# Gate and up of a feed-forward layer by seven block products instead of eight (Strassen's scheme), results through DRAM, then down

## The chip, the cores and the metric

One core of a Trainium2 chip runs the whole program. The metric is the device time in microseconds of one execution; the time before is the median of three executions.

## What is computed

One step of a hybrid decoder layer for 2048 prompt tokens and 32 sample tokens, model width 1024, feed-forward width 2816 (22 tiles of 128), all in float32. The change touches its last third:

```
x = x + g1 * (mixed @ w_out)
h = rms_norm(x, norm2_g) * (1 + sc2) + sh2
ff = silu(h @ w_gate) * (h @ w_up)
x = x + g2 * (ff @ w_down)
y = rms_norm(x, final_g)
```

A float32 product is made on TensorE from two reduced-precision pieces of each operand, hi (a copy rounded to fp32r by ScalarE) and lo (the rest, by a subtraction on GpSimd or VectorE): hi·hi + hi·lo + lo·hi, three matmuls for one.

## The kernel before, in words

`phase_out` (L1562) goes over the 16 token tiles of 128 in the order 8 to 15, then 0 to 7 (`order`, L1578). For a tile, `stage1` (48 matmuls `oz` of 512 columns, L1645 to L1647) makes the output projection; `stage1e` (L1658 to L1665) adds the residual, squares, and writes the normalised tile `oxn`; in the next round `stage2` transposes it (`oT`, L1673), scales it into `oh`, and splits it into hi and lo (L1684 to L1691). Tiles 0 to 7 stay in SBUF (`h2`), tiles 8 to 15 go to DRAM (`d_h2`). In the last round `next(ff)` puts the first gate and up work, `gate_up(0, 0)`, between the last `stage1` and the last `stage2`.

`phase_ff` goes over two halves of 1024 tokens and, in each, over the 22 ff tiles. For a tile, `gate_up` works on three chunks of tokens (256, 384, 384; 288 for the first chunk of the second half, with the sample tokens). For a chunk it makes two products of 8 blocks of the contraction and 3 matmuls each, that is 2 x 24 matmuls `fg` (L1908, L1909, L1911), then SiLU on ScalarE, a multiplication on VectorE (L1915), and the hi/lo split (L1916, L1917). The down product of the tile before, `down` (three matmuls `fd` of 512 columns for each of 16 accumulators, L1948 to L1950, and an addition on VectorE, L1957), stands between the chunks. Weights arrive in pieces of 256 KB through SyncE's queue and are split by `split_next` (L1857 ScalarE, L1858 GpSimd).

At the end of each half the accumulators are multiplied by g2 and the residual is added, ahead of the last sum (`pre`, L1986 VectorE and L1987 GpSimd, 128 x 1024 each). `last_sum`, `fin_rms` and `fin_out` then finish tile by tile; at the very end this is the list `LAST`. The order of instructions on each engine is the order in which the program writes them, and each engine takes its own strictly in that order. Each engine's DMAs are issued by SyncE in the order of the program too.

PSUM has two pools of four buffers: `R["a"]` for projections and gate/up, `R["b"]` for transposes and down.

Of the kernel before, what the change touches and what calls it, by code (L numbers as in the profile page):

```python
# [7 lines left out]
F32 = mybir.dt.float32  # L8
# [11 lines left out]
HT = 1024  # L20
LOG_G = [__import__("math").log1p(-(2.0 ** (-5.0 - h))) for h in range(NRH)]
# [75 lines left out]
def hybrid_step(ctx: ExitStack, tc: tile.TileContext, i: dict, o: dict):  # L97
# [57 lines left out]
    d_h2 = [dram.tile([DM, T + NS], F32R, name=f"d_h2{a}") for a in range(2)]  # L155
# [1403 lines left out]

    CH = [(0, 256), (256, 384), (640, 384)]  # L1560

    def phase_out(R, ff):  # L1562
# [5 lines left out]
        h_p = P("oh", 1)  # L1568
# [9 lines left out]
        order = list(range(8, 16)) + list(range(8))  # L1578
# [88 lines left out]
        def stage2(t):  # L1667
# [13 lines left out]
            if t < 8:  # L1681
                c = (t + 1) // 3
                hh, hl = (a[:, :, t * 128 - CH[c][0]:t * 128 - CH[c][0] + 128] for a in R["h2"][c])
                act.copy(hh, h)  # L1684
                pool.tensor_tensor(hl, h, f32(hh), ALU.subtract)
                return
            for g in range(2):
                hv = h[:, 4 * g:4 * g + 4]
                hh, hl = (R["gu"].tile([128, 4, 128], F32R, tag=f"g{a}", name=f"oh{a}") for a in range(2))
                act.copy(hh, hv)  # L1690
                pool.tensor_tensor(hl, hv, f32(hh), ALU.subtract)  # L1691
                for a, s in enumerate((hh, hl)):
                    later(d_h2[a][512 * g:512 * g + 512, t * 128:(t + 1) * 128].rearrange("(k p) n -> p k n", p=128), s)
# [3 lines left out]
        def half(tag, name):  # L1697
            return [R["gu"].tile([128, 4, 128], F32, tag=tag, name=name)[0:NS].rearrange("p k n -> p (k n)") for _ in range(2)]

        def sample0():  # L1700
            SM["g"] = half("g0", "g1s")
            SM["xs"] = half("g1", "oxs")
            for c in range(2):
                cs = slice(c * 512, c * 512 + 512)
                for b in range(NB):
                    dma(SM["g"][c][4 * b:4 * b + 4, :], d_g[1 + b:2 + b, 0, cs].to_broadcast([4, 512]))
                dma(SM["xs"][c], i["x_sample"].rearrange("b t d -> (b t) d")[:, cs])
# [26 lines left out]
        def sample1x():  # L1734
            for c in range(2):
                dve.tensor_scalar(SM["xn"][c], SM["x1"][c], SM["s3"][:, 4:5], None, ALU.mult)

        def sample2():
            xn = SM["xn"]
            pt = R["b"].tile([128, 512], F32, tag="b", name="oTs")  # L1740
            v = pt[:, 0:256].rearrange("p (k b t) -> p k b t", k=8, t=4)
            for k in range(8):
                pe.transpose(pt[:, k * 32:(k + 1) * 32], xn[k // 4][:, k % 4 * 128:k % 4 * 128 + 128], ident[0:NS, 0:NS])
            t, hh, hl = (R["wr"].tile([128, 4, 128], F32 if x == 0 else F32R, tag="g", name=f"ohs{x}").rearrange("p k n -> p (k n)")[:, 0:256]
                         .rearrange("p (k n) -> p k n", k=8) for x in range(3))
# [6 lines left out]
            for a, s in enumerate((hh, hl)):  # L1752
                dma(d_h2[a][:, T:T + NS].rearrange("(k p) n -> p k n", p=128), s)
# [398 lines left out]
```

## Time and profile before

| what | value |
|---|---|
| median of 3 executions | 3173.06 us (3171.83 to 3179.8) |
| profiled execution | 3173.09 us, of which its span 3171.3 us |
| mean granted TensorE clock | 0.965 |
| PE busy | 3086.2 us, 97% of the span |
| DVE / POOL / ACT busy | 1333.2 / 1255.7 / 944.9 us |
| on the chain that ended last | PE 85% of the span |

The profile lists each engine's busy time, then the chain of work that ended last. PE is TensorE, DVE VectorE, ACT ScalarE, POOL GpSimd, SP SyncE. An operation is written out<-in with its shape. Matmuls overlap in their records: what one costs is the distance from start to start, not its listed length. A time in square brackets behind a row is the idle time ahead of it and what ended it.

### The profile page before, as it was taken

What the parts mean: (1) busy time and instruction counts of PE and PEld (TensorE: products, weight loads), DVE (VectorE), ACT (ScalarE), POOL (GpSimd) and SP (SyncE); (2) the same over time, 40 slices, a digit from 0 to 9 for tenths busy, and PEclk for the clock granted to TensorE, in tenths of its full rate; (3) what the DMA queues carried; (4) which work ended last, traced back from release to release, by engine and by line L of the source; (5) the groups of instructions that cost most, each with busy time, mean ns of one, the idle gap of its engine ahead of it and who ended that gap; (6) DMA issues with size and microseconds to landing.
All of it is one profiled execution on the core that took longest, in us unless ns stands there. A gap on an engine that the chain in (4) does not pass through costs nothing.

```text
span 3171.3 us, 45654 instructions
## 1 busy us (share of the span) xinstructions
PE 3086.2 (97%) x17690; PEld 2747.4 (87%) x17690; DVE 1333.2 (42%) x2772; ACT 944.9 (30%) x1869; POOL 1255.7 (40%) x1093
## 2 busy tenths in 40 slices
PE   8999999999999997989999999999999999999997
PEld 4777888889999997768889999999998999999996
DVE  6424533124343334664552333333363344334447
ACT  5333422204444462463342111111123111111112
POOL 4546836302333342564343333333354333223337
PEclk9999999997898798999999999999999999999999
DMA  6555745627544428774642111121153111111122
GB/s 230 162 163 169 226 124 166 196 74 170 129 109 102 99 59 241 245 252 149 191 130 60 41 54 47 40 60 41 50 191 116 40 47 51 44 41 53 48 72 83
DMA packets 354035, 361.91 MB, mean 114 GB/s; under 512 B 36701, under 2 KB 266909, under 8 KB 350678
## 3 DMA queue, kind: packets, MB, share of 16 engines
q1 hardware_dynamic: 352888, 357.92, 38.2%
q8 instruction: 139, 2.28, 0.3%
q10 hardware_dynamic: 930, 1.07, 0.1%
q14 instruction: 78, 0.64, 0.1%
HBM read 274.41 MB, written 84.50 MB: 113 GB/s over the span
## 4 chain that ended last, share of the span: by engine, by line
PE 85%; DVE 3%; issue 3%; DMA 3%; POOL 2%; ACT 1%; SPq 0%; POOLq 0%; DVEq 0%; ACTq 0%
PE fg L1908 10%; PE fg L1909 10%; PE fg L1911 10%; PE fd L1949 5%; PE z L518 5%; PE fd L1950 5%; PE fd L1948 5%; PE z L519 5%; PE z L523 5%; PE aB L874 3%; PE aB L873 3%; PE aS L806 2%; PE aS L808 2%; PE aB L858 2%; PE oz L1645 1%
## 5 line engine op out<-in xcount | busy, mean ns | idle before, releaser
L1909 PE MATMUL fg<-h,g 128*128 128x384 f32 (+2 forms) x2112 | 653.1, 320 | 0.0
L1908 PE MATMUL fg<-h,g 128*128 128x384 f32 (+2 forms) x2112 | 652.0, 320 | 0.0
L1917 POOL TENSOR_TENSOR f<-sg,f 128x256 fp32r<-128x256 f32 x132 | 127.9, 969 | 948.1 <-ACT f L1916 948.1
L1957 DVE TENSOR_TENSOR acc<-fd,acc 128x512 f32<-128x512 f32 x640 | 437.2, 691 | 13.1 <-PE fd L1950 7.3
L1915 DVE TENSOR_TENSOR sg<-fg,sg 128x256 f32<-128x256 f32 (+1 forms) x132 | 68.5, 519 | 866.0 <-PE fg L1911 863.3
L1908 PEld LDWEIGHTS fg<-h,g 128*128 128x128 f32 x2112 | 397.5, 188 | 6.1
L1909 PEld LDWEIGHTS fg<-h,g 128*128 128x128 f32 x2112 | 397.1, 188 | 5.1
L1911 PE MATMUL fg<-h,g 128*128 128x384 f32 (+2 forms) x2112 | 374.8, 319 | 0.0
L1911 PEld LDWEIGHTS fg<-h,g 128*128 128x128 f32 x2112 | 340.2, 188 | 0.0
L518 PE MATMUL z<-w,hh 128*128 128x512 f32 x768 | 310.7, 405 | 2.0 <-ACT w L313 1.7
L519 PE MATMUL z<-w,hh 128*128 128x512 f32 x768 | 305.4, 398 | 0.9 <-DVE w L314 0.9
L1948 PE MATMUL fd<-d,f 128*128 128x512 f32 x704 | 275.2, 391 | 7.5 <-ACT acc L1955 3.4
L880 POOL TENSOR_TENSOR pl<-p,ph 128x512 fp32r<-128x512 f32 (+2 forms) x128 | 155.4, 1214 | 315.0 <-ACT ph L879 233.8
L1950 PE MATMUL fd<-d,f 128*128 128x512 f32 x704 | 276.1, 392 | 2.8 <-POOL f L1917 2.8
L1949 PE MATMUL fd<-d,f 128*128 128x512 f32 x704 | 276.2, 392 | 1.2 <-POOL d L1858 1.2
L1914 ACT ACTIVATE sg<-fg 128x256 f32<-128x256 f32 (+1 forms) x132 | 60.8, 460 | 664.9 <-PE fg L1911 664.9
L812 DVE CUSTOM_DVE_ANT_0 junk<-aS,mask 128x256 f32<-128x256 f32 (+1 forms) x384 | 121.1, 363 | 298.4 <-PE aS L808 297.2
L1858 POOL TENSOR_TENSOR g<-gr,g 128x512 fp32r<-128x512 f32 x176 | 229.3, 1325 | 0.0
L1916 ACT CAST f<-sg 128x256 fp32r<-128x256 f32 x132 | 63.0, 477 | 504.1 <-DVE sg L1915 504.1
L523 PE MATMUL z<-w,hl 128*128 128x512 f32 x768 | 193.1, 393 | 0.0
L518 PEld LDWEIGHTS z<-w,hh 128*128 128x128 f32 x768 | 147.0, 191 | 34.9 <-ACT w L313 2.1
L519 PEld LDWEIGHTS z<-w,hh 128*128 128x128 f32 x768 | 147.1, 192 | 31.7 <-DVE w L314 1.5
(337 smaller groups left out, 6103.9 us busy)
## 6 DMA issues: line engine op xcount, KB each, us to landing
raw<-in_w_in SPq DMA_DIRECT2D x96, 256.0 KB
gr<-in_w_gate SPq DMA_DIRECT2D x88, 256.0 KB
gr<-in_w_up SPq DMA_DIRECT2D x88, 256.0 KB
dr<-in_w_down SPq DMA_DIRECT2D x88, 256.0 KB
ar<-in_w_ada SPq DMA_DIRECT2D x32, 512.0 KB
d_qk<-g SPq DMA_DIRECT2D x64, 256.0 KB
v<-d_v SPq DMA_DIRECT2D x16, 1024.0 KB
sk<-in_cache_attn_k SPq DMA_DIRECT2D x56, 256.0 KB
```

The lines of the kernel that those rows point to most:

```text
L518: pe.matmul(ps, hh[:, k, :], hi[:, k, :], start=(k == 0), stop=False)
L519: pe.matmul(ps, hh[:, k, :], lo[:, k, :], start=False, stop=False)
L523: pe.matmul(ps, hl[:, k, :], hi[:, k, :], start=False, stop=(k == 7))
L880: (dve if gi in DV[h] else pool).tensor_tensor(lo[:, 0:off], p[:, 0:off], f32(hi[:, 0:off]), ALU.subtract)
L1858: (eng or pool).tensor_tensor(lo, t, f32(hi), ALU.subtract)
L1908: pe.matmul(ps[:, 0:w], wh, xh[:, k], start=(k == 0), stop=False)
L1909: pe.matmul(ps[:, 0:w], wh, xl[:, k], start=False, stop=False)
L1911: pe.matmul(ps[:, 0:w], ww[k // 4][1][:, k % 4], xh[:, k], start=False, stop=(k == 7))
L1948: pe.matmul(ps, f[0][:, tt], d[0][:, cs], start=(q == 0), stop=False)
L1949: pe.matmul(ps, f[0][:, tt], d[1][:, cs], start=False, stop=False)
L1950: pe.matmul(ps, f[1][:, tt], d[0][:, cs], start=False, stop=(q == len(ns) - 1))
L1957: dve.tensor_tensor(acc, ps, acc, ALU.add)
```

## The change

Gate and up become block products after Strassen (in Winograd's form, with seven products for eight). For each pair of ff tiles (11 pairs) and each pass over the tokens, the weight is seen as 2 x 2 blocks (two halves of the contraction, two ff tiles) and the activations as 2 x 2 blocks (two halves of the contraction, two blocks of tokens). Seven products of 4 x 3 = 12 matmuls each replace eight of 12. There are three passes over the tokens with blocks of 384, 384 and 272 columns (`NCH`; the last with 16 sample tokens in each block).

- In `phase_out` the tile order changes so that tiles come in pairs (t, t+3; in the last pass t, t+2). After a pair's second tile, `combine` makes four sums of 128 x 512 on DVE, and `blocks` splits seven operands into hi and lo (ScalarE, GpSimd). Four of them for pass 0 stay in SBUF; all others go to DRAM (`d_B`), fourteen writes of 256 KB for a pair (six in pass 0). The last three of a pair are split one round later (`rest`).
- `g_build` makes the weight's seven operands for each pair, pass and matrix: four sums of 128 x 512 on DVE and seven splits. The subtraction of a split is on GpSimd; in the last pass two of seven are on VectorE. They are built five products ahead. The weights are read once a pass, three times in all instead of twice.
- `product` combines the seven products with seven additions on DVE that read PSUM, for each matrix; the four results go through SiLU and a multiplication, and are written to DRAM as `d_ff`.
- Down follows when gate and up are done: it reads `d_ff` and w_down back, splits them (`d_build`), and adds two ff tiles at a time in PSUM (6 matmuls for one addition into the accumulator instead of 3). The finish of each half is as before, without gate and up between its steps.
- `gate_up(0, 0)` no longer stands ahead of the last `stage2`.

```diff
+NCH = (384, 384, 272)
-        order = list(range(8, 16)) + list(range(8))
+        order = [0, 3, 1, 4, 2, 5, 6, 9, 7, 10, 8, 11, 12, 14, 13, 15]
+        def combine(b11, b21, b12, b22, t1, t2, t4):
+            dve.tensor_tensor(t1, b12, b11, ALU.subtract)
+            dve.tensor_tensor(t2, b22, t1, ALU.subtract)
+            dve.tensor_tensor(b12, b22, b12, ALU.subtract)
+            dve.tensor_tensor(t4, b21, t2, ALU.subtract)
+            return [b11, t2, b12, t1, b21, t4, b22]
...
+        def g_build(s):
+            q, idx = divmod(s, 14)
+            x, w = divmod(idx, 2)
...
+            if x == 1:
+                s1, s2 = tmp(1), tmp(2)
+                dve.tensor_tensor(s1, a21, a22, ALU.add)
+                dve.tensor_tensor(s2, s1, a11, ALU.subtract)
+            if x == 2:
+                dve.tensor_tensor(tmp(3), a11, a21, ALU.subtract)
+            if x == 4:
+                dve.tensor_tensor(tmp(4), a12, GT[w, 2], ALU.subtract)
...
+            act.copy(hi, src)
+            eng = dve if q >= 2 * NP_ and x in (2, 5) else pool
+            eng.tensor_tensor(lo, src, f32(hi), ALU.subtract)
...
+        def product(s):
...
+            for k in range(4):
+                pe.matmul(ps, hi[:, k], xh[:, k], start=(k == 0), stop=False)
+                pe.matmul(ps, hi[:, k], xl[:, k], start=False, stop=False)
+            for k in range(4):
+                pe.matmul(ps, lo[:, k], xh[:, k], start=False, stop=(k == 3))
+            put_off()
+            if x == 0:
+                act.copy(t, ps)
+            elif x < 3:
+                dve.tensor_tensor(t, ps, PT[w, x - 1], ALU.add)
+            else:
+                dve.tensor_tensor(v, ps, PT[w, (2, 0, 2, 1)[x - 3]], ALU.add)
+                if x == 3:
+                    dve.tensor_tensor(t, ps, t, ALU.add)
+                if w == 0:
+                    act.activation(SG[out], v, AF.Silu)
+                else:
+                    def end():
+                        dve.tensor_tensor(sg, v, sg, ALU.mult)
+                        later(d_ff[f][:, t0:t0 + m], sg[:, 0:m])
...
+        for s in range(14 * NG):
+            product(s)
+            while built[0] < s + 1 + LEAD:
+                build()
...
+                for x in range(2):
+                    d, f = DO[q, 2 + x, c], DO[q, x, t // 4]
+                    pe.matmul(ps, f[0][:, tt], d[0], start=(x == 0), stop=False)
+                    pe.matmul(ps, f[0][:, tt], d[1], start=False, stop=False)
+                    pe.matmul(ps, f[1][:, tt], d[0], start=False, stop=(x == 1))
```

Three places where the order of instructions matters below. First TensorE's at the end of `phase_out`; `oz` is the last projection, `oT` the transposes of the last tile, `fg` gate and up. Before:

```order
L1645 MATMUL oz<-wo_14043,m_16363 128x512
L1646 MATMUL oz<-wo_14044,m_16363 128x512
L1647 MATMUL oz<-wo_14043,m_16364 128x512
L1908 MATMUL fg<-h_14832,g_16300 128x256
L1909 MATMUL fg<-h_14833,g_16300 128x256
```

and in the changed kernel:

```order
L1645 MATMUL oz<-wo_14069,m_16465 128x512
L1646 MATMUL oz<-wo_14070,m_16465 128x512
L1647 MATMUL oz<-wo_14069,m_16466 128x512
L1673 MATMUL oT<-ident,oxn 128x128 x8
L1980 MATMUL fg<-B_14870,op_14863 128x384
```

The transposes of the last tile now follow its projection at once; the first gate product stands behind them.

Second SyncE's DMAs at the same place in the changed kernel; `B40` to `B61` are activation blocks of pass 0, `op` and `B70` hold the last pair's blocks for the last pass, and `raw3` is the first piece that the up matrix needs for its second operand (with index 3 of the products):

```order
L110 DMA B60_16659<-d_B00_71 128x1536
L110 DMA B61_16660<-d_B01_72 128x1536
L110 DMA d_x1_70<-x1_16529 128x1024
L110 DMA d_B20_75<-op00_14855 128x4x128
L110 DMA d_B21_76<-op01_14856 128x4x128
L110 DMA d_B20_75<-op10_14857 128x4x128
...
L110 DMA d_B21_76<-B71_16662 128x4x128
L110 DMA d_x1_70<-x1_16630 128x1024
L110 DMA raw3_16734<-in_w_up 128x4x256
L110 DMA raw4_16735<-in_w_gate 128x4x256
```

The piece `raw3` stands behind six reads of 768 KB and fourteen writes of 256 KB.

Third VectorE's order in the last pass of the changed kernel; L1901 to L1906 are sums of weight blocks, L1911 the low half of a split, L1990 and L1997 additions from PSUM, L2007 the multiplication behind SiLU:

```order
L2007 TENSOR_TENSOR sg_23255<-fc_23274,sg_23255 128x272
L1997 TENSOR_TENSOR sg_23296<-fg_23282,fu_23099 128x272
L1901 TENSOR_TENSOR s1_23299<-raw1_14853,raw3_16734 128x512
L1902 TENSOR_TENSOR s2_23300<-s1_23299,raw1_14853 128x512
L1997 TENSOR_TENSOR fc_23318<-fg_23305,fu_23117 128x272
L1904 TENSOR_TENSOR s3_23320<-raw0_14852 128x512
L1911 TENSOR_TENSOR op01_14856<-s3_23320,op00_14855 128x512
L2007 TENSOR_TENSOR sg_23296<-fc_23318,sg_23296 128x272
L1904 TENSOR_TENSOR s3_23340<-raw1_14853 128x512
L1911 TENSOR_TENSOR op11_14858<-s3_23340,op10_14857 128x512
```

Where VectorE had one operation on gate and up for each 24 pairs of matmuls, it now has about two operations for each product of 12 matmuls, and over half of them take both operands from SBUF.

## Rows read from the trace of the kernel before

**Rows 1.** The page: the span, and each engine's busy time, share and instructions.

```profile
span 3171.3 us, 45654 instructions
PE 3086.2 (97%) x17690; PEld 2747.4 (87%) x17690; DVE 1333.2 (42%) x2772; ACT 944.9 (30%) x1869; POOL 1255.7 (40%) x1093
```

**Rows 2.** Busy time by stretch of the span: start and end us, length, then busy us (and instructions) of PE, PEld, DVE, ACT and POOL, the granted clock, the DMA share, GB/s. Two stretches of the feed-forward stage in the first half, then the change of halves and one behind it.

```profile
2200.00:2300.00 100.00, 100.00 (x578) 94.09 (x578) 37.51 (x57) 17.79 (x36) 30.93 (x27) 1.00 0.16 48
2300.00:2400.00 100.00, 97.83 (x548) 91.28 (x547) 61.86 (x70) 25.30 (x50) 60.17 (x46) 1.00 0.58 188
2400.00:2500.00 100.00, 96.60 (x529) 89.11 (x528) 29.41 (x43) 26.04 (x55) 31.78 (x34) 0.98 0.22 69
2600.00:2700.00 100.00, 100.00 (x564) 93.42 (x564) 38.61 (x60) 16.69 (x36) 30.07 (x29) 1.00 0.16 48
```

**Rows 3.** Instructions of PE in order of time (start us, length us, engine, line, operation): the first gate product of 256 columns, the transposes behind its 48 matmuls; a group of 24 matmuls of 384 columns, the 18 of 512 behind it and the next; a group of 24 of 288 columns and what follows.

```profile
1637.76 0.28 PE L1908 MATMUL fg<-h,g 128*128 128x256 f32 x1
1643.41 1.03 PE L1673 MATMUL oT<-ident,oxn 128*128 128x128 f32 x8
...
1908.45 0.33 PE L1908 MATMUL fg<-h,g 128*128 128x384 f32 x1
1912.61 0.39 PE L1948 MATMUL fd<-d,f 128*128 128x512 f32 x1
1916.73 0.33 PE L1908 MATMUL fg<-h,g 128*128 128x384 f32 x1
...
2400.66 0.29 PE L1908 MATMUL fg<-h,g 128*128 128x288 f32 x1
2403.86 0.39 PE L1948 MATMUL fd<-d,f 128*128 128x512 f32 x1
```

**Rows 4.** Groups of instructions by line and shape, the whole span: engine, operation, shapes and count, then busy us, mean ns of one, and the idle time before them.

```profile
L1957 DVE TENSOR_TENSOR acc<-fd,acc 128x512 f32<-128x512 f32 x640 | 437.2, 691 | 13.1 <-PE fd L1950 7.3
L1915 DVE TENSOR_TENSOR sg<-fg,sg 128x384 f32<-128x384 f32 x88 | 49.1, 558 | 645.1 <-PE fg L1911 642.5 <-ACT sg L1914 2.7
L1915 DVE TENSOR_TENSOR sg<-fg,sg 128x288 f32<-128x288 f32 x22 | 10.0, 456 | 111.6 <-PE fg L1911 111.6
L1659 DVE TENSOR_TENSOR x<-x,ox 128x512 f32<-128x512 f32 x32 | 37.0, 1157 | 1.1
L1727 DVE TENSOR_TENSOR x1s<-x1s,oxs 32x512 f32<-32x512 f32 x2 | 1.4, 678 | 0.1
L1858 POOL TENSOR_TENSOR g<-gr,g 128x512 fp32r<-128x512 f32 x176 | 229.3, 1325 | 0.0
L1691 POOL TENSOR_TENSOR oh<-oh,oh 128x512 fp32r<-128x512 f32 x16 | 24.4, 1546 | 52.2 <-ACT oh L1690 52.2
L1987 POOL TENSOR_TENSOR acc<-acc,fx 128x1024 f32<-128x1024 f32 x16 | 40.3, 2526 | 10.6 <-DVE acc L1986 8.1 <-DVE acc L1957 2.4
L1857 ACT CAST g<-gr 128x512 fp32r<-128x512 f32 x176 | 100.3, 617 | 0.4 <-DMA gr<-in_w_gate 0.4
```

**Rows 5.** Instructions in order of time at the end of the first half: a multiplication of the accumulators on DVE beside GpSimd's work, the GpSimd instruction that ran at its start, and the same multiplication with less beside it.

```profile
2338.67 3.36 DVE L1986 TENSOR_TENSOR acc<-acc,g2b 128x1024 f32<-128x1024 f32 x1
...
2338.55 2.39 POOL L1987 TENSOR_TENSOR acc<-acc,fx 128x1024 f32<-128x1024 f32 x1
...
2362.84 1.35 DVE L1986 TENSOR_TENSOR acc<-acc,g2b 128x1024 f32<-128x1024 f32 x1
```

**Rows 6.** Instructions in order of time for one tile of `phase_out`: the transposes of one tile and of the next, the normalised tile between them, and GpSimd's two splits.

```profile
1501.60 1.03 PE L1673 MATMUL oT<-ident,oxn 128*128 128x128 f32 x8
1513.90 1.03 PE L1673 MATMUL oT<-ident,oxn 128*128 128x128 f32 x8
...
1508.93 0.75 DVE L1665 TENSOR_SCALAR oxn<-x,os 128x1024 f32<-128x1024 f32 x1 [2.26 <-POOL os L1664]
...
1504.83 3.00 POOL L1691 TENSOR_TENSOR oh<-oh,oh 128x512 fp32r<-128x512 f32 x2 [6.57 <-ACT oh L1690]
```

**Rows 7.** Instructions in order of time at the end of `phase_out`: the last transposes but one, the last matmul of the projection, the last normalised tile.

```profile
1632.47 1.66 PE L1673 MATMUL oT<-ident,oxn 128*128 128x128 f32 x8 [2.27 <-DVE oxn L1665]
1637.53 0.40 PE L1647 MATMUL oz<-wo,m 128*128 128x512 f32 x1
...
1641.90 0.76 DVE L1665 TENSOR_SCALAR oxn<-x,os 128x1024 f32<-128x1024 f32 x1 [1.97 <-POOL os L1664]
```

**Rows 8.** Busy time by stretch, as rows 2: ten microseconds in which the blocks of the second half were read (rows of 1 to 1.5 KB), and four in which transposed tiles were written (rows of 512 bytes).

```profile
2370.00:2380.00 10.00, 10.00 (x54) 9.32 (x53) 3.12 (x5) 4.35 (x9) 7.39 (x8) 1.00 1.06 374
1564.00:1568.00 4.00, 4.00 (x19) 3.32 (x18) 2.04 (x3) 1.80 (x6) 0.18 (x1) 1.00 0.96 305
```

**Rows 9.** Instructions of PE behind the change of halves, in order of time: an idle time and the matmuls of 384 columns that came after it.

```profile
2410.12 0.50 PE L1948 MATMUL fd<-d,f 128*128 128x512 f32 x1 [3.36 <-ACT acc L1955]
2412.06 0.52 PE L1908 MATMUL fg<-h,g 128*128 128x384 f32 x1
2414.30 0.43 PE L1909 MATMUL fg<-h,g 128*128 128x384 f32 x1
```

**Rows 10.** Instructions in order of time at the end: the last sums' first matmul, the first multiplication of its result, and VectorE's last operation.

```profile
3118.05 0.39 PE L1948 MATMUL fd<-d,f 128*128 128x512 f32 x1
3121.19 0.69 DVE L1998 TENSOR_TENSOR ft<-fd,g2b 128x512 f32<-128x512 f32 x1 [2.32 <-PE fd L1950]
3166.40 1.28 DVE L2028 SCALAR_TENSOR_TENSOR fsp<-acc,fs,fgb 128x1024 f32<-128x1024 f32 x1 [0.72 <-POOL fs L2020]
```

**Rows 11.** Busy time by stretch, as rows 2: ten microseconds of the attention stage.

```profile
970.00:980.00 10.00, 10.00 (x56) 9.80 (x56) 2.67 (x9) 3.28 (x6) 2.57 (x2) 0.50 1.02 202
```

More of the change, by code (lines that the diff above doesn't have):

```diff
@@ L1680, in stage2 @@
                         dve.tensor_scalar(h[:, kk], v, modA[1][:, kk, 0:1], modB[1][:, kk, 0:1], ALU.mult, ALU.add)
[L1681 to L1685, printed above, removed]
-                return
[L1687 to L1693, printed above, removed]
+            p = min(t // 6, 2)
@@ L1695, in phase_out @@
         SM = {}
-        def half(tag, name):
-            return [R["gu"].tile([128, 4, 128], F32, tag=tag, name=name)[0:NS].rearrange("p k n -> p (k n)") for _ in range(2)]
         def sample0():
[L1701 to L1707, printed above, removed]
+            SM["g"], SM["xs"] = (r[0:NS] for r in R["raw"][0:2])
@@ L1814, in phase_out @@
         stage2(order[15])
+        rest()
+        put_out()
         settle()
@@ new lines, in phase_ff @@
+        yield
+        build()
+        yield
+        P, close_g = group("left")
+        more = P("fmore", 1)
+        BO += [[more.tile([128, 4, 384], F32R, name=f"B{x}{a}") for a in range(2)] for x in range(4, 8)]
+        R["late"] = [[a[:, :, 128 * x:128 * x + 128] for a in BO[7]] for x in range(3)]
+        for x in range(4, 7):
+            b_load(0, x)
+        yield
+        Q, close_gw = group("right")
+        gw = Q("fgw", 1)
+        RAW += [gw.tile([128, DM], F32, name=f"raw{x}") for x in range(3, 6)]
@@ new lines, in phase_ff @@
+        for s in range(14 * NG):
+            q, idx = divmod(s, 14)
+            product(s)
+            if s == 8:
+                b_load(1, 0)
+            if idx == 8 and q == NP_:
+                b_load(2, 0)
+            while built[0] < s + 1 + LEAD:
+                build()
+            if s == 14 * (NG - 1):
+                for x in range(4):
+                    d_raw(0, x)
+        put_off()
+        settle()
+        close_g()
+        R["close_B"]()
+        P, close_down = group("right")
@@ L1926, in phase_ff, with down @@
-        gate_up(0, 0)
-        yield
-        P, close_right = group("right")
-        accp = P("facc", 1)
-        accs = [accp.tile([128, DM], F32, name=f"acc{t}") for t in range(8)]
-        acs = one.tile([64, DM], F32, name="accs")
-        def down(ns, t, c, raw=False):
-            f0 = seqf[ns[0]][1]
+        while built[0] < 14 * NG + 8:
+            build()
+        bank = [0]
+        def down(q, t, c, raw=False):
+            bank[0] ^= 1
+            ps = R["ab"[bank[0]]].tile([128, 512], F32, tag="ab"[bank[0]], name="fd")
@@ L1936, in down @@
             cs = slice(c * 512, c * 512 + 512)
[L1937 removed]
             if t == 8:
[L1939 removed]
+                for x in range(2):
                     for a in range(2):
[L1941 to L1942 removed]
+                        pe.matmul(ps[0:64], DO[q, "s", x], DO[q, 2 + x, c][a], start=(x == 0 and a == 0), stop=(x == 1 and a == 1))
@@ L1957, in down @@
                 dve.tensor_tensor(acc, ps, acc, ALU.add)
-        spare = [one.tile([128, DM], F32, name=f"fsp{i}") for i in range(2)]
         X = {"as": spare[0][0:NS], "g2s": spare[1][0:NS]}
```

438 lines of the change are left out of this document (247 added, 191 removed).

## The prediction
> **What bounds the kernel now.** I read the page's head first: TensorE is busy 97% of the span [rows 1], so the time is its instructions plus few gaps. The stretches come next [rows 2]: in the feed-forward stage it is busy throughout at the full clock, DVE a third of the time, POOL a third, the DMA engines 16%. The order in time [rows 3] gives the price of a matmul, from start to start: 24 of 384 columns take 1912.61 - 1908.45 = 4.16 us, 0.1733 each; 18 of 512 take 4.12, 0.229 each; 24 of 288 take 3.20, 0.1333 each; 48 of 256 take 5.65, 0.1177 each. So columns are what is paid, and fewer of them is time saved as long as the other engines keep up. They have to do far more here, so the rest of the argument is about them.
>
> **Gate and up on TensorE.** Before, 22 tiles x 48 matmuls x 0.1177 and x 0.1333, and 22 x 192 x 0.1733: 124 + 141 + 732 = 997 us. Now 33 rounds (a round is one pair of ff tiles in one pass) x 168 matmuls, of 384, 384 and 272 columns. For 272 I estimate 0.1255, between the groups of 256 and 288 [rows 3]. 1848 x (0.1733 + 0.1733 + 0.1255) = 872 us. **-125 us.** Down has 2112 matmuls of 512 columns in both, at no change. A round lasts 168 x 0.1733 = 29.1 us in the first two passes, 21.1 us in the third. Of the 48 matmuls taken to be on the path before, the 8.3 us of the last `gate_up` stood inside the final chain of DVE, POOL and ACT (3118.05 to the end, 53 us [rows 10]), where I let its loss save 3 only: **+5**.
>
> **The sums and splits of a round, passes 0 and 1.** DVE: 8 weight sums with both operands in SBUF. Such an operation takes 0.678 us alone (L1727) and 1.157 on average beside POOL (L1659) [rows 4]; I take 1.157. Then 14 additions from PSUM at 0.558 and 4 multiplications of 384 columns at 0.558 + 0.47 for the same delay: 9.3 + 7.8 + 4.1 = 21.2 us. POOL: 14 splits at 1.325 (L1858) to 1.546 (L1691) = 18.6 to 21.6. ACT: 14 copies at 0.617 and six smaller operations, some 12. All below 29.1, so I cost them at nothing; TensorE covers them, with 7 us to spare. Without that cover each microsecond over 29.1 would cost 22 us.
>
> **The third pass.** TensorE gives only 21.1 us. DVE now has 12 operations with two SBUF operands, four of them low halves: 12 x 1.157 = 13.9; 14 additions from PSUM at 0.456 (L1915 of 288 columns, for 272) = 6.4; 4 multiplications at 0.456 + 0.47 = 3.7. Together 24.0 us, 2.9 more than TensorE, x 11 = 32; the five operands built ahead and eight PSUM buffers hide some 8 of it once. **+24** (0 if DVE is not slowed: 16.3 us; upper end in the rivals). Why DVE is slow beside POOL, the order in time shows [rows 5]: the multiplication that began at 2338.67, just behind a POOL addition of 2.39 us, took 3.36 us, one with less beside it 1.35; the difference is the rest of the POOL instruction. The Trainium skill (SBUF — State Buffer, SBUF: two separate sides) speaks against this change: VectorE with two SBUF inputs and GpSimd take turns on a shared port pair, an exclusive lock held for the whole instruction. Rows 5 agree. By it alone the round's lock time would be 10 x 1.325 + 12 x 0.678 + 4 x 0.456 = 23.2 us, some 2 over TensorE, and the sum 9 us less than with my 24.0.
>
> **`phase_out`.** A tile's round is 12.3 us, from 1501.60 to 1513.90; its normalised tile is ready 8.1 us after the transposes [rows 6], so 4.2 us are spare. A pair's second tile now has, ahead of that, four DVE sums (2.7 to 4.6 us) and four splits on POOL instead of two (+3.1 us at 1.546), partly beside each other: some 5.9, so 1.7 us of waiting for each of 7 pairs. In the last round the transposes come 2.7 us earlier (one group of 12 matmuls) and already waited 2.27 [rows 7]; 3 us more. **+15** (0 if DVE and POOL overlap wholly; 35 if transfers come late too: a pair moves 6.7 MB in 24.6 us where 305 GB/s [rows 8] gives 22).
>
> **Entry into gate and up.** Before, TensorE went from the last projection straight into 48 gate matmuls [rows 3, 7]. Now it waits for the normalised tile until 1641.9 + 0.8 [rows 7], 5 us; after the transposes it has two products, then the third and fourth need POOL and a weight piece. POOL must first split the last pair's seven blocks: 3 us for scaling and the first sums, then 7 x 1.546 = 10.8, so to about 1657. SyncE cannot issue `raw3` before the writes of these blocks, and if transfers land in the order of issue it follows 4.7 MB of reads at 374 GB/s (12.6 us), 3.7 MB of writes at 305 (12 us) [rows 8] and 0.5 MB of the residual: 1665. With two sums and a copy the fourth product starts at about 1669, against 1645 without waits: 24 us, and the first matmuls after it come at the lower clock. That costs some 2 us: after an idle time of 3.36 us, 7 of 384 columns took 2.24 us, 0.32 each [rows 9]. **+27** (18 if `raw3` does not queue behind the writes, 38 if all reads and writes run at 250 GB/s).
>
> **Between the stages.** At a pass change 9.4 MB of blocks arrive over some 50 us at 374 GB/s where each is used 29 us after it is asked for: nothing. `d_ff`, and weights read a third time, add up to 2.9 MB a round, 100 GB/s: nothing, at the DMA shares of rows 2. Into down: the last three splits of the first pair and new buffers, **+4** (1 to 10).
>
> **The finish of the halves.** `pre` puts on each tile a multiplication on DVE (1.35 alone) and a POOL addition of 2.53 us [rows 4, 5], beside a split of 1.33: 5.2 us one after the other. Before, this had 33 us of matmuls for eight tiles, and still cost: 548 + 529 matmuls where 571 + 564 would be usual [rows 2], 57 x 0.176 = 10 us. Now it has 8 x 2.74 = 21.9 us. DVE ends them 20 us late and the next round, at some 3.2 us a tile with output and splits, 25 us late; TensorE, with eight PSUM buffers at most four tiles (11 us) ahead, loses 14, and 3 to its clock. 17 us, that is **+7** net (-5 to 15). Second half: 8 x 5.2 + 5.6 for the sample tile = 47 against 23.7 on TensorE, and the final chain waits for DVE's end: **+22** (8 to 30; before, gate and up covered it).
>
> **The sum.** -125 + 5 + 24 + 15 + 27 + 4 + 7 + 22 = -21. From the profiled execution's 3173.09, which is the median's 3173.06 within 0.1: **3152 us**, 0.7% faster. The unknowns add up to some 25 either way: 3130 to 3178 for this case.
>
> **Rivals.**
> *The other engines keep up.* The sums then wait little: third pass 0 instead of 24, entry 19. 3152 - 24 - 8 = 3120. For it: DVE alone would need 16.3 us of 21.1, and operands are built ahead. Against: rows 5, and the mean of L1659.
> *DVE waits a whole POOL instruction at each split.* Third pass: 16.3 + 10 x 1.325 = 29.6 us a round, (29.6 - 21.1) x 11 - 7 = 87 instead of 24: 3215, slower. It decides from 25.8 us a round on, where the third pass costs 45 and the gain is gone. For it: in-order DVE sits between POOL's splits, and the low halves wait for ACT's copy. Against: 14 additions from PSUM need no lock and can lie beside POOL.
> *Waiting TensorE runs at 1.2 GHz.* In a stretch of the attention stage it was listed busy throughout, at a clock of 0.50 [rows 11]. If four rounds of the third pass ran so, at 0.1255 x 0.32 / 0.1733 = 0.232 us for a matmul, 39 us a round: 4 x (39 - 24) = +60, 3212. The Trainium skill (TensorE: Matmul & The Clock Gate, A second HAM failure mode: psum-queue depth-cycling) tells of such a case, where small waits between groups let the clock fall again and again. Against: at 2300 to 2400 the clock stayed at 1.00 with 98% busy [rows 2].
> That the eighth product is still made can be excluded: in the order of instructions there are 5544 gate and up matmuls, 3 x 1848, where 6336 were.
>
> **How the numbers follow.** About 0.3% (9.5 us) is what a measurement of this kernel can tell from no change. My forecast has 0.50 (0.37 of it below 3163.6, 0.13 within), the first rival 0.25, the second 0.16, the third 0.09. Faster 0.62, same 0.13, slower 0.25. For 8 in 10 the range goes from 3105, a little under the first rival, to 3205; the two slow ones begin where the gain ends, so about half of their 0.25 lies inside.
>
> **What would show it.** Right: `fg` in 5544 matmuls at 0.173 and 0.125 from start to start; rounds of 29 us in passes 0 and 1 with TensorE busy, 24 in pass 2 with DVE never idle and its sums at 1.1 us; an idle time of about 20 us ahead of the fourth product, ended by a DMA; TensorE waiting for DVE or POOL at the end of both halves. Wrong: rounds of over 30 us in the first passes; pass 2 at 21 (first rival) or over 26 (second); a granted clock below 0.9 in pass 2 (third); waits of over 3 us for each pair in `phase_out`; or transfers late at the pass changes.

## The result, and the profile after

The changed kernel takes 3146.86 us (median of five executions, 3145.01 to 3154.42), the kernel before beside it 3171.83: a ratio of 0.9927, 95% interval 0.9906 to 0.9949. The forecast was 3152. So the sum came out 5 us too high; single terms are further off, and the profile shows which.

The head of the page first, to be set against [rows 1]: TensorE lost 792 matmuls and 105 us, DVE gained 443 us of work and GpSimd 363.

```profile
span 3145.0 us, 46998 instructions
PE 2981.4 (95%) x16898; PEld 2631.0 (84%) x16898; DVE 1776.3 (56%) x3271; ACT 1143.0 (36%) x2215; POOL 1618.9 (51%) x1279
```

The stretches next (columns as [rows 2]): the first passes, the third pass, the change to down, the end of the first half, and the round ahead of the last sums.

```profile
1900.00:2000.00 100.00, 100.00 (x577) 100.00 (x576) 68.25 (x89) 36.50 (x70) 68.81 (x50) 1.00 0.41 132
2400.00:2500.00 100.00, 96.65 (x734) 93.05 (x733) 88.89 (x133) 43.77 (x89) 64.18 (x44) 1.00 0.41 114
2580.00:2600.00 20.00, 16.92 (x75) 13.25 (x74) 5.23 (x5) 11.57 (x22) 12.06 (x10) 1.00 0.74 277
2800.00:2820.00 20.00, 10.55 (x35) 7.26 (x34) 19.10 (x15) 3.34 (x7) 16.91 (x8) 0.69 0.41 131
3060.00:3080.00 20.00, 19.15 (x84) 14.83 (x82) 19.83 (x17) 0.00 (x0) 20.00 (x11) 1.00 0.36 106
3080.00:3100.00 20.00, 13.81 (x49) 9.71 (x49) 15.01 (x11) 1.20 (x2) 18.66 (x8) 0.83 0.14 40
```

Passes 0 and 1 are what was forecast: TensorE busy throughout, 577 matmuls in 100 us, DVE at 68%. In the third pass 734 matmuls stand where the price of 0.1255 gives 797. At 2800 to 2820 there are 35 of 88.

A profile is one execution, and the place where a stage begins moves between executions. So stages are compared by their own length. The summary of the output projection on TensorE (line, count, min/median/max ns, first and last start), for the kernel before, then for the changed one:

```profile
L1645 PE MATMUL oz<-wo,m x256: 387/389/774, 1420.9 to 1637.1; 128*128 128x512 f32 x128
L1647 PE MATMUL oz<-wo,m x256: 388/389/628, 1421.3 to 1637.5; 128*128 128x512 f32 x128
```

```profile
L1645 PE MATMUL oz<-wo,m x256: 387/389/776, 1412.8 to 1651.8; 128*128 128x512 f32 x128
L1647 PE MATMUL oz<-wo,m x256: 387/389/628, 1413.3 to 1652.3; 128*128 128x512 f32 x128
```

Up to its first matmul the changed kernel was 8.1 us ahead, in a part of the program that both share; experiments with the same code there began anywhere from 1410.8 to 1428.3. From first to last it took 239.5 us for 216.6. With that, the differences by stage (us, + is slower):

| term | forecast | measured | from |
|---|---|---|---|
| matmuls of gate and up | -125 | -122 | 0.1740 each in passes 0 and 1 for 0.1733 |
| last gate_up in the final chain | +5 | +8 | final chain 50.1 us in both |
| third pass | +24 | +16 | 248.3 us for 1848 x 0.1255 = 231.9 |
| phase_out | +15 | +23 | 239.5 - 216.6 |
| entry | +27 | +36 | 1652.5 to 1699.6, with 11.4 us of work in it |
| into down | +4 | +3 | two waits on PE, 2.4 and 0.7 |
| first half's finish | +7 | +3 | 56 matmuls short x 0.2285 = 12.8, less the 10 of before |
| second half's finish | +22 | +14 | 37.8 us for a round of 23.8 |
| sum | -21 | -19 | spans -26.3, without the 8.1 ahead of it -18.2 |

**phase_out's end.** In the last round, in order of time: ACT, POOL, DVE (two rows), PE. In brackets, the idle time before the instruction and what ended it.

```profile
1650.62 0.62 ACT L1711 CAST op<-oh 128x512 fp32r<-128x512 f32 x1 [5.73 <-DMA d_B<-op]
...
1651.59 1.29 POOL L1712 TENSOR_TENSOR op<-oh,op 128x512 fp32r<-128x512 f32 x1 [5.28 <-DMA d_B<-op]
...
1652.92 1.36 DVE L1680 TENSOR_SCALAR oh<-oT,modA,modB 128x128 f32<-128x128 f32 x4 [5.82 <-POOL op L1712]
1659.50 0.75 DVE L1665 TENSOR_SCALAR oxn<-x,os 128x1024 f32<-128x1024 f32 x1 [2.22 <-POOL os L1664]
...
1660.31 1.97 PE L1673 MATMUL oT<-ident,oxn 128*128 128x128 f32 x8 [7.66 <-DVE oxn L1665]
```

Read upwards, TensorE waited 7.66 us for the normalised tile; DVE had stood 5.82 us at the activations of the tile before, whose buffer the split still read; POOL and ACT had waited 5 us to split, since the operand buffer was not yet written out. The last three blocks of a pair use the buffers of its first three. My estimate had the sums and splits, not this wait: from the first projection to the last, ACT has 37 us of it and POOL 33. The wait of 7.66 us itself stands behind the last projection, so the table has it under the entry.

The first wait for an operand buffer ends at 1552.6. Ahead of that, behind each of the first four pairs, TensorE waits 1.64 to 1.68 us for the normalised tile, with no such wait in front of it; for example:

```profile
1470.82 1.09 PE L1673 MATMUL oT<-ident,oxn 128*128 128x128 f32 x8 [1.68 <-DVE oxn L1665]
```

After 1552 TensorE's waits for this tile are 2.13, 3.65, 0.96 and 4.14 us.

**The entry.** The third and the fourth product, the sum that the fourth waits for, and SyncE's issues (x8 is eight in a row, from the first start to the last end):

```profile
1673.29 0.69 PE L1980 MATMUL fg<-B,op 128*128 128x384 f32 x1 [5.84 <-ACT op L1909]
1692.64 0.69 PE L1980 MATMUL fg<-B,op 128*128 128x384 f32 x1 [14.75 <-ACT op L1909]
...
1690.52 0.69 DVE L1901 TENSOR_TENSOR s<-raw,raw 128x512 f32<-128x512 f32 x1 [17.94 <-DMA raw<-in_w_up]
...
1664.42 13.58 SPq L110 DMA_DIRECT2D d_B<-op  x8
1678.10 5.38 SPq L110 DMA_DIRECT2D d_B<-B  x6
1684.51 0.71 SPq L110 DMA_DIRECT2D raw<-in_w_up  x1
```

The chain is the forecast one: `raw3` behind the writes. It is issued 32.2 us after the last projection, the product starts 40.4 us after it, where I had 31.5, since the writes wait for POOL, and POOL's splits of the last pair ended 22.7 us after it instead of 19.5. TensorE's granted clock was 0.57 over 1680 to 1700; the twelve matmuls of the fourth product took 4.0 us at the lower level, 1.2 GHz, for 2.1 at 2.4.

**The third pass.** Groups of DVE in 2350 to 2550 (columns as [rows 4]), then part of one round in order of time, DVE and POOL:

```profile
L2007 DVE TENSOR_TENSOR sg<-fc,sg 128x272 f32<-128x272 f32 x34 | 26.8, 790 | 1.2 <-ACT sg L2002 0.8
L1906 DVE TENSOR_TENSOR s<-raw,s 128x512 f32<-128x512 f32 x18 | 25.3, 1408 | 0.0
L1904 DVE TENSOR_TENSOR s<-raw 128x512 f32<-128x512 f32 x18 | 12.2, 680 | 0.0
L1911 DVE TENSOR_TENSOR op<-s,op 128x512 fp32r<-128x512 f32 x18 | 14.7, 814 | 13.6 <-ACT op L1909 13.6
L1997 DVE TENSOR_TENSOR fc<-fg,fu 128x272 f32<-128x272 f32 x26 | 11.3, 433 | 0.9 <-PE fg L1983 0.9
```

```profile
2425.84 0.68 DVE L1904 TENSOR_TENSOR s<-raw 128x512 f32<-128x512 f32 x1
...
2431.22 1.39 DVE L1906 TENSOR_TENSOR s<-raw,s 128x512 f32<-128x512 f32 x1
2432.54 0.43 DVE L1990 TENSOR_TENSOR fu<-fg,fu 128x272 f32<-128x272 f32 x1
2432.89 1.42 DVE L1906 TENSOR_TENSOR s<-raw,s 128x512 f32<-128x512 f32 x1
...
2430.77 2.99 POOL L1911 TENSOR_TENSOR op<-s,op 128x512 fp32r<-128x512 f32 x2 [3.10 <-ACT op L1909]
2433.72 3.45 POOL L1911 TENSOR_TENSOR op<-raw,op 128x512 fp32r<-128x512 f32 x2
```

A sum takes 0.68 us alone (2425.84) and 1.4 beside a POOL split; the two of 1.39 and 1.42 stand beside POOL's splits, and the addition from PSUM between them keeps its 0.43. Lengths of neighbours overlap: the operation at 2432.54 is 0.43 long and the next starts 0.35 later.

**The end.** The first multiplication of the accumulators, the first one behind the last sums, and DVE's last operation, as [rows 10]:

```profile
3057.10 1.22 DVE L2146 TENSOR_TENSOR acc<-acc,g2b 128x1024 f32<-128x1024 f32 x1
...
3094.91 1.27 DVE L2159 TENSOR_TENSOR ft<-fd,g2b 128x512 f32<-128x512 f32 x2
...
3140.23 1.28 DVE L2189 SCALAR_TENSOR_TENSOR fsp<-acc,fs,fgb 128x1024 f32<-128x1024 f32 x1 [0.72 <-POOL fs L2181]
```

From 3094.91 to the span's end it is 50.1 us, and from 3121.19 to 3171.3 [rows 10] it was 50.1 as well: taking a whole `gate_up` out of that chain saved nothing.

### The profile page after: what moved, and what is told of

It is laid out like the page before. It is cut to its first block, busy times and chain, and to the rows that moved or that the text cites. A ratio compares the mean times of both kernels' runs of the same rounds, so it can differ in the third digit from the quotient of the medians.

```text
span 3145.0 us, 46998 instructions
## 1 busy us (share of the span) xinstructions
PE 2981.4 (95%) x16898; PEld 2631.0 (84%) x16898; DVE 1776.3 (56%) x3271; ACT 1143.0 (36%) x2215; POOL 1618.9 (51%) x1279
## 4 chain that ended last, share of the span: by engine, by line
PE 77%; POOL 6%; issue 5%; DVE 4%; DMA 4%; SPq 1%; ACT 1%; POOLq 0%; ACTq 0%; DVEq 0%
PE fg L1983 8%; PE fg L1980 8%; PE fg L1981 8%; PE z L521 5%; PE z L522 5%; PE z L526 5%; PE fd L2110 4%; PE fd L2111 4%; PE fd L2109 4%; PE aB L877 3%; PE aB L876 3%; PE aS L809 2%; PE aS L811 2%; POOL op L1911 2%; PE aB L861 1%
## 5 line engine op out<-in xcount | busy, mean ns | idle before, releaser
L1980 PE MATMUL fg<-B,op 128*128 128x384 f32 (+1 forms) x1848 | 579.0, 323 | 25.7 <-ACT op L1909 25.7
L1981 PE MATMUL fg<-B,op 128*128 128x384 f32 (+1 forms) x1848 | 576.0, 321 | 0.0
L1911 POOL TENSOR_TENSOR op<-s,op 128x512 fp32r<-128x512 f32 x242 | 336.6, 1405 | 261.7 <-ACT op L1909 219.1
L1980 PEld LDWEIGHTS fg<-B,op 128*128 128x128 f32 x1848 | 349.2, 189 | 30.1 <-ACT op L1909 29.7
L1983 PE MATMUL fg<-B,op 128*128 128x384 f32 (+1 forms) x1848 | 370.4, 322 | 1.1
L1981 PEld LDWEIGHTS fg<-B,op 128*128 128x128 f32 x1848 | 349.6, 189 | 0.0
L1983 PEld LDWEIGHTS fg<-B,op 128*128 128x128 f32 x1848 | 306.1, 188 | 5.3 <-POOL op L1911 4.7
L2051 POOL TENSOR_TENSOR op<-raw,op 128x512 fp32r<-128x512 f32 x132 | 188.9, 1447 | 209.8 <-ACT op L2050 196.2
L2118 DVE TENSOR_TENSOR acc<-fd,acc 128x512 f32<-128x512 f32 x304 | 207.8, 689 | 154.8 <-PE fd L2111 154.5
L2110 PE MATMUL fd<-op,op 128*128 128x512 f32 x704 | 278.2, 395 | 16.5 <-POOL op L2051 16.5
L2109 PE MATMUL fd<-op,op 128*128 128x512 f32 x704 | 277.8, 395 | 10.8 <-DVE ft L2159 5.3
L1911 POOL TENSOR_TENSOR op<-raw,op 128x512 fp32r<-128x512 f32 x176 | 261.1, 1499 | 52.0 <-ACT op L1909 51.9
L2111 PE MATMUL fd<-op,op 128*128 128x512 f32 x704 | 277.4, 394 | 0.0
L1909 ACT CAST op<-s 128x512 fp32r<-128x512 f32 x264 | 160.3, 620 | 245.8 <-DVE s L1902 167.2
L2050 ACT CAST op<-raw 128x512 fp32r<-128x512 f32 x176 | 101.8, 621 | 306.1 <-issue 212.2
L2002 ACT ACTIVATE sg<-sg 128x384 f32<-128x384 f32 (+1 forms) x132 | 65.4, 495 | 323.1 <-DVE sg L1997 323.0
L521 PEld LDWEIGHTS z<-w,hh 128*128 128x128 f32 x768 | 146.5, 191 | 35.0 <-ACT w L316 2.1
```

The source lines that it names most:

```text
L521: pe.matmul(ps, hh[:, k, :], hi[:, k, :], start=(k == 0), stop=False)
L1911: eng.tensor_tensor(lo, src, f32(hi), ALU.subtract)
L1980: pe.matmul(ps, hi[:, k], xh[:, k], start=(k == 0), stop=False)
L1981: pe.matmul(ps, hi[:, k], xl[:, k], start=False, stop=False)
L1983: pe.matmul(ps, lo[:, k], xh[:, k], start=False, stop=(k == 3))
L2051: (dve if idx in (3, 7) else pool).tensor_tensor(lo, src, f32(hi), ALU.subtract)
```

## The experiments

Stage lengths in the profiled executions, us: `phase_out` from its first to its last projection; from there to the first matmul of 272 columns; the third pass to the first down matmul; from there to the span's end.

| kernel | phase_out | entry, passes 0 and 1 | third pass | down | median |
|---|---|---|---|---|---|
| changed kernel | 239.5 | 680.1 | 248.3 | 564.4 | 3146.9 |
| e1 early piece | 240.3 | 664.7 | 248.2 | 565.8 | 3134.7 |
| e2 all splits on POOL | 239.3 | 679.4 | 256.6 | 564.7 | 3158.0 |
| e3 no sums in pass 2 | 239.8 | 678.6 | 232.2 | 562.9 | 3133.0 |
| e4 half the writes | 235.5 | 667.9 | 248.3 | 564.2 | 3135.4 |
| e5 six buffers in turn | 233.2 | 678.5 | 248.1 | 565.8 | 3141.4 |
| e6 sums twice | 239.3 | 700.0 | 248.2 | 565.5 | 3171.9 |
| e8 scaled down weights | 240.3 | 681.5 | 248.1 | 521.7 | 3105.9 |
| e10 three together | 233.4 | 662.3 | 248.1 | 521.6 | 3084.0 |
| e11 three, mended | 240.0 | 660.8 | 248.1 | 521.1 | 3088.6 |
| e12 six splits on DVE | 239.6 | 678.5 | 255.6 | 566.1 | 3159.5 |
| e13 turn shifted | 232.6 | 663.9 | 248.1 | 521.0 | 3091.5 |

Lengths of stages that an edit does not touch agree within 3.2 us, mostly within 1; medians carry the shifts of the earlier stages besides, so small effects are read from the lengths.

**e1.** A buffer of its own for `raw3`, issued ahead of the blocks' reads:

```
+        R["raw3"] = more.tile([128, DM], F32, name="raw3e")
+        g_load(0, 3)
...
-        g_load(0, 3)
```

> The fourth weight piece (raw3) gets a buffer of its own and is issued ahead of the block reads. Theory: TensorE's 14.75 us ahead of the fourth product stand only for this piece, which SyncE issued at 1684.5, behind the writes of the last pair's blocks, while POOL had finished that pair's splits at 1675. Then the fourth product follows the third: 13 to 16 us less, 3131 to 3134. Rival: the transfers are the limit there (DMA share 0.97 and more from 1640 to 1700), each byte moved ahead delays another, and the wait comes back at the products that need the blocks read last: -3 to +3, 3144 to 3150.

3134.66 us, ratio to before 0.9898 (0.9882 to 0.9913). The stretch behind `phase_out` is 15.4 us shorter, as the theory has it. TensorE's waits there now end with the third product; the fourth (second row) follows without idle time:

```profile
1680.89 0.69 PE L1981 MATMUL fg<-B,op 128*128 128x384 f32 x1 [5.63 <-ACT op L1909]
1686.17 0.52 PE L1981 MATMUL fg<-B,op 128*128 128x384 f32 x1
```

The transfers were not the limit: the piece stood in the wrong place in the queue.

**e2, e3, e12: the third pass.** e2 gives all low halves to POOL, e3 leaves the sums out (a block itself stands in their place, so its results are other numbers), e12 gives two more low halves to DVE; the edits in this order:

```
-            eng = dve if q >= 2 * NP_ and x in (2, 5) else pool
+            eng = pool
```

```
+            if q >= 2 * NP_:
+                for n in range(1, 5):
+                    GT[w, n] = a11
```

```
-            eng = dve if q >= 2 * NP_ and x in (2, 5) else pool
+            eng = dve if q >= 2 * NP_ and x in (2, 4, 5) else pool
```

> In the third pass POOL makes all 14 splits of a round, DVE none. Theory (DVE is the bound there by its number of operations with two SBUF operands): DVE falls from 20 us a round to 16, POOL stands at 14 x 1.41 = 19.8 of TensorE's 21.1, rounds go from 22.6 to 21.2: 10 to 15 us less, 3132 to 3137. Rival (DVE's sums are stretched by the POOL instructions beside them, and four more of these cost what DVE is spared): sums at 1.4 us and more for 1.1, rounds of 22.5 to 24, that is 0 to 15 us more, 3147 to 3162.

> Leaves out the eight weight sums of a round in the third pass (the operands are then made from a block itself); splits and additions from PSUM stay. Theory: DVE falls from 20 to 11 us a round, and the whole loss of the pass (248 us for 232 of matmuls) goes: rounds of 21.1, 14 to 16 us less, 3131 to 3133. Rival: POOL's and ACT's chain (copy, then split) holds TensorE as well, and half of the loss stays: 5 to 9 us less, 3138 to 3142.

> In the third pass DVE makes six low halves of a round for four, POOL eight for ten. With none on DVE the pass had become 8 us longer, though DVE had less to do. If each POOL instruction costs DVE a wait, and four was merely on the near side of the best division, six gives 0 to 8 us less, 3139 to 3147. If DVE's number of operations counts, as in my 24.0 us a round, two more of 0.8 to 1.1 in a round that DVE fills to 89% give 10 to 22 us more, 3157 to 3169.

3157.98, 3132.96 and 3159.49 us. The same 100 us of each, columns as above, in this order:

```profile
2400.00:2500.00 100.00, 96.03 (x720) 91.33 (x719) 84.90 (x110) 41.23 (x83) 86.55 (x61) 1.00 0.41 118
```

```profile
2400.00:2500.00 100.00, 100.00 (x799) 100.00 (x798) 60.59 (x104) 46.28 (x96) 60.78 (x47) 1.00 0.43 125
```

```profile
2400.00:2500.00 100.00, 94.89 (x718) 91.08 (x716) 90.28 (x137) 41.71 (x85) 50.88 (x36) 1.00 0.39 115
```

Without the sums the pass takes 232.2 us, the price of its matmuls, with POOL still at 61% and 799 matmuls at 2400 to 2500: the whole 16 us belong to the sums. Whether by their time on DVE or because copy and split have to wait for them, e3 does not tell apart, and more operands built ahead were not tried. Yet the other way round, four splits fewer on DVE made the pass 8.3 us longer, though DVE fell to 85%, with POOL at 87% and DVE's multiplication at 1.33 us for 0.79. And two more made it 7.3 us longer, with DVE at 90% and POOL at 51%. So neither engine's own count decides by itself. With DVE's busy share at 85 to 90%, products are late, and the reading that fits all three is that moving a split trades DVE's operation against the time that DVE stands beside POOL's. Of 0, 4 and 6, four is the best. The Trainium skill (Perfetto Trace Analysis, Optimizing Scalar/DVE Operations) warns that moving operations between these two engines might not help, since they share a port; here both directions cost 7 to 8 us, which agrees. My expectation for e12, 10 to 22 us by the count, was too large in the pass itself; its median lies 12.6 above, and in its profiled execution `phase_out` began 6.6 us later than in the changed kernel's, in a part that both share.

**e4 and e5: the writes.** e4 writes the high halves alone (and reads them twice), e5 takes operand buffers in turn. In e5 the sample's block, which keeps its fixed buffer, is overwritten before it is written out, so the sample columns hold other data; instructions and transfers are the same. The two edits in this order:

```
-                for a in range(2):
-                    OUT.append((d_B[p][a][:, x, :, qs], dst[a]))
+                OUT.append((d_B[p][0][:, x, :, qs], dst[0]))
```

```
+                if p < 2:
+                    dst = R["ops"][SLOT[0] % 6]
+                    SLOT[0] += 1
```

> Leaves out the writes of the low halves of the activation blocks (the reads take the high half for both, as many bytes as before), 8 MB for 16 MB of such writes. Theory: the end of phase_out (14.8 us later than before) and the entry are late by transfers, since ACT and POOL waited 4 to 6 us for operand buffers not yet written out, with the DMA share at 0.94: the last projection starts 8 to 12 us earlier and the entry is 5 to 8 us shorter, 13 to 20 in all, 3127 to 3134. Rival, the one of my prediction: the DVE sums and the POOL splits ahead of the normalised tile make phase_out late; then it stays, and only the entry gains: 0 to 6 us less, 3141 to 3147.

> The blocks of the first two thirds of the tokens go through six operand buffers in turn, where the last three of a pair had to reuse the first three buffers of the same pair. Theory: phase_out (239.5 us from its first projection to its last, 216.6 before) is late because ACT and POOL wait for buffers whose writes to DRAM are still under way (35 and 33 us of such waits), and DVE's next activations wait for POOL's splits: these waits fall by more than half, and phase_out to 228 to 233: 6 to 11 us less, 3136 to 3141. Rival (four more DVE sums and seven POOL splits for four a pair, as predicted, make the normalised tile late): the waits for writes fall, and phase_out stays at 237 to 240: 0 to 3 us less, 3144 to 3147.

3135.37 and 3141.42 us. e5 shortens `phase_out` by 6.3 us, at the lower edge of the theory:

```profile
L1645 PE MATMUL oz<-wo,m x256: 387/389/777, 1428.3 to 1661.1; 128*128 128x512 f32 x128
L1647 PE MATMUL oz<-wo,m x256: 388/390/628, 1428.7 to 1661.5; 128*128 128x512 f32 x128
```

From the first projection to the last, ACT's waits for such writes fall from 37 us to 20, POOL's from 33 to 12. About 17 of the 23 us stay, but they are not the sums and splits alone, which I had put at 15: in the last round ACT still waits 5.91 us for a buffer. e4 gains only 4.0 us there but 12.2 at the entry, where the writes stood ahead of `raw3`. So both causes hold: the sums and splits by the four waits of some 1.65 us each, which e5 leaves as they were, the buffers by the 6.3 us. How the rest divides between them no run shows.

**e6: the cover of the first two passes.**

```
                 dve.tensor_tensor(s1, a21, a22, ALU.add)
+                if q < 2 * NP_:
+                    dve.tensor_tensor(s1, a21, a22, ALU.add)
...
```

> Makes each weight sum of passes 0 and 1 twice. Theory of my prediction: DVE is busy there 20 of 29.1 us a round, TensorE covers it. Eight more operations at 1.12 make 29 us, all the cover: 0 to 40 us more, 3147 to 3187, with DVE at 95% and more. Rival (DVE's sums are stretched by the POOL instructions beside them, and chains of sum, copy and split make operands late well before DVE is full): over 40 us more, above 3187. If it is free (3144 to 3150) the cover was larger than I counted.

3171.88 us; the stretch with passes 0 and 1 is 19.9 us longer, 0.9 a round. The stretch 1800 to 2000:

```profile
1800.00:2000.00 200.00, 198.28 (x1120) 193.71 (x1119) 177.21 (x228) 69.04 (x131) 134.12 (x93) 1.00 0.31 96
```

It is in the range, but not by the expected way: DVE is at 89%, not 95%, and TensorE already waits. So the cover ends somewhere between the 70% of the changed kernel in this stretch, where TensorE does not wait, and 89%, about the share of the third pass. The eight operations raise DVE by 6.4 us a round, not by the 9 of eight at 1.12: others stand less beside POOL's instructions, the multiplication for one, at 0.72 us for 1.23.

**e8: the finishes.** w_down's rows are multiplied by g2 from the second pair on, the first pair's result in its eviction; the residual is added to one tile a round; the sample's gate is divided by g2 once.

```
-            if x > 1 and h == 0 and q == NP_ - 1:
+            if x > 1 and h == 0 and q:
                 dve.tensor_tensor(DR[q, x], DR[q, x], g2, ALU.mult)
...
-                    if m == NP_ - 2:
-                        pre(hf, t)
+                    if 0 < m < 9 and t == 1 or t == 8 and m == NP_ - 2:
+                        pre(hf, m - 1 if t == 1 else 8)
```

> The rows of w_down are multiplied by the gate g2 from the second pair on, so that the accumulators need no multiplication in the last but one round, and the residual is added to one tile a round; the sample's gate is divided by g2. Theory: the finishes cost 12 us in the first half and 14 us in the second since each tile there has a DVE multiplication and a POOL addition that make each other wait, and the last 50 us are a chain of the same engines: all of the first two and 10 to 17 us of the last go, 33 to 43 us less, 3104 to 3114. Rival: two more DVE operations of 1024 columns a round beside POOL's splits make the rounds of down longer or operands late, and the chain at the end is held by ACT and POOL: 0 to 15 us less, 3132 to 3147.

3105.89 us, ratio 0.9783 (0.9759 to 0.9806). The end of the first half, and DVE at the end: the first addition of the last round and the last operation:

```profile
2800.00:2820.00 20.00, 20.00 (x89) 16.42 (x88) 14.40 (x20) 6.27 (x13) 9.74 (x12) 1.00 0.14 49
...
3074.63 1.27 DVE L2120 TENSOR_TENSOR acc<-fd,acc 128x512 f32<-128x512 f32 x2
...
3102.96 1.28 DVE L2186 SCALAR_TENSOR_TENSOR fsp<-acc,fs,fgb 128x1024 f32<-128x1024 f32 x1 [0.72 <-POOL fs L2178]
```

TensorE has 89 matmuls where it had 35, and from 3074.63 to the end it is 33.1 us for 50.1. Down is 42.7 us shorter: 12.8 and 14 of the finishes, 17 of the final chain, as the theory added it up. The two multiplications a round (1.50 us each) cost nothing visible: DVE stands at 69%.

**e10, e11, e13: the three together.** e10 is e1, e5 and e8; in e11 the sample's block takes the next buffer in turn (in e10 it is overwritten as in e5); e13 starts the turn one buffer earlier; the two edits:

```
-            hi, lo = (a.rearrange("p k n -> p (k n)")[:, 0:448].rearrange("p (x k n) -> p x k n", x=7, k=4) for a in R["ops"][3])
+            hi, lo = (a.rearrange("p k n -> p (k n)")[:, 0:448].rearrange("p (x k n) -> p x k n", x=7, k=4) for a in R["ops"][SLOT[0] % 6])
+            SLOT[0] += 1
```

```
-        SLOT = [0]
+        SLOT = [5]
```

> The early weight piece, the six buffers in turn and the scaled down weights together. If the three act at separate places, as the theory has it, the sum of their single gains: 15 + 6 to 11 + 33 to 43, that is 3078 to 3093. Rival: an earlier end of phase_out only lengthens the wait at the entry, since transfers are the limit from 1600 to 1700; then the buffers add nothing here, 3090 to 3100.

> As the run of all three changes before, but the sample's block too takes the next operand buffer in turn, so that no block is overwritten before it is written out. Its instructions are the same: 3078 to 3093 as there, near 3084.

> As the mended kernel, but the turn through the six buffers starts at the sixth instead of the first. With the sample in the turn, the last block of one pair had fallen into the buffer that the next pair, which uses fixed ones, needs first, and ACT waited 5.74 us for its write at 1637. If such a wait is what phase_out's end hangs on, it goes from 240.0 to 233 to 235 us as in the two runs without the sample in the turn, and the kernel to 3080 to 3086. If those 6 us were scatter between executions, it stays at 239 to 240: 3085 to 3091.

3083.97, 3088.59 and 3091.46 us; ratios to before 0.9725 (0.9703 to 0.9748), 0.9737 (0.9720 to 0.9755) and 0.9738 (0.9711 to 0.9766). The gains add up: the lengths of e1, e5 and e8 fall by 15.4, 6.3 and 42.7 us singly, those of e10 by 66.9 together. In e11 the turn's order put one block into a buffer that the next pair needs first, and `phase_out` was back at 240 us; ACT's wait there, and the first and last projection of e13:

```profile
1637.70 0.62 ACT L1712 CAST op<-oh 128x512 fp32r<-128x512 f32 x1 [5.74 <-DMA d_B<-op]
```

```profile
L1645 PE MATMUL oz<-wo,m x256: 387/389/775, 1416.6 to 1648.7; 128*128 128x512 f32 x128
L1647 PE MATMUL oz<-wo,m x256: 388/389/628, 1417.0 to 1649.2; 128*128 128x512 f32 x128
```

With the turn shifted `phase_out` takes 232.6 us again, so the 6 to 7 us are the buffers' and not scatter. The entry is 3 us longer (663.9 for 660.8), as much as untouched stages scatter, and in the medians e13 and e11 cannot be told apart. Both beat the changed kernel and the kernel before, by some 57 and 82 us.

## Why the prediction was right, term by term

The sum was right because the mechanism was: fewer columns, paid back at the seams where other engines or the queue come last. The sizes were off by up to 9 us, in both directions: four terms were too small by 23 us together, four too large by 21. That these cancel is luck, and so is part of the last 5 us, since the profiled execution was 8.1 us ahead before the change began. Two slips in the working weigh 1 us at most: 548 + 529 matmuls are 58 fewer than 571 + 564, not 57, and the entry's parts add up to 26, not 27.

*The matmuls* cost what the rows gave: 0.1255 is exact (e3's pass is 232.2 us for 231.9).

*The third pass* was sized at +24 and is +16. That DVE's sums make it is shown by e3. The step that was too large is the sum of DVE's lengths, 24.0 us: they measure 22.2 a round, neighbours overlap, and DVE is busy 20 of the 22.6 us of a round, idle for the rest, mostly behind ACT's copies. The eight microseconds that I let the operands built ahead hide are not needed to explain it. The second rival's 29.6 us did not come, and no run supports a full wait at every split; but its mechanism is in the rows, where the sum takes 0.68 alone and 1.4 beside a split. The Trainium skill (SBUF — State Buffer, SBUF: two separate sides) has this as an exclusive lock for the whole instruction; the rows agree for pairs of SBUF operands. By it alone I had estimated 23.2 us of lock for a round of the third pass; the same estimate gives 25.8 with all splits on POOL (14 x 1.325 + 8 x 0.678 + 4 x 0.456) and 21.9 with six on DVE. Measured are 22.6, 23.3 and 23.2: the lock cannot be held for all of the recorded length, and with six on DVE it is not what decides.

*`phase_out`*: the step "some 5.9, so 1.7 us of waiting for each of 7 pairs" holds behind the first four pairs (1.64 to 1.68 us). Missing was the wait for operand buffers still being written, which sets in behind these; I had it only in the upper end, as late transfers. Turning through six buffers takes 6 to 7 us of it away (e5, e13). Two of the later waits, 3.65 and 4.14 us, are over the 3 us that the prediction had named as a sign of being wrong.

*The entry*: "SyncE cannot issue `raw3` before the writes of these blocks" is shown by e1, 15 us of it. The term was too small since the writes follow POOL's splits, which came 3 us later than I counted, and since they took SyncE until 1683.5. The rest of the 36 us are the waits for the normalised tile and the third product's operand, and the lower clock: with the early piece the third and fourth product still ran at 0.32 us a matmul, until 1689.

*Into down* was right. *The finishes* were sized at 7 net and 22, and are 3 and 14: I took a tile's 5.2 us as one chain of DVE and POOL; a tile took 37.8 / 9 = 4.2, as POOL's addition lies beside DVE's additions from PSUM. e8 shows that most of these two and 17 us of the final chain are what `pre` and the last multiplications cost. That the last `gate_up` would save 3 us in that chain was wrong: 50.1 and 50.1, nothing.

*Passes 0 and 1 at nothing* holds within 2.6 us, but the cover is thinner than "7 us to spare" says: e6 loses 20 us with DVE at 89%.

The first rival (the other engines keep up) fails at the entry and in the third pass, the third (a low clock in the third pass) at the granted clock of 1.00 there.

## What to carry to other kernels

A scheme that saves TensorE columns is paid for at the seams: ask in which order the queue carries the first operands of the next stage (one load of 512 KB moved gave 15 us), and which buffers must have drained before the last splits of a stage. Do not count on the last tenth of an in-order engine whose operations wait for other engines in between: here TensorE waited with DVE at 85 to 90% busy, and did not at 61 and 70%; nothing between was measured. Before work is traded between two engines that hinder each other, look for work that can leave the pinch altogether: a gate folded into the weights and a residual spread over the rounds gave 43 us.

## What was not expected

With code that is alike up to there, `phase_out` began between 1410.8 and 1428.3 us in twelve profiled executions, a scatter as large as most of the terms.

Taking splits off DVE, whose sums make the loss of the third pass, made that pass longer; I had this only as a rival. Four splits fewer took 8.3 us more, two splits more 7.3, so the best of the three lies between them.
